# Nearest-neighbour upsampling by two: rows in two blocks of 236 and 276 per partition, ten stores in place of nine, a last load of 9 KB

## The chip, the cores and the metric

The kernel runs on one core of one Trainium2 chip. The metric is device microseconds of that core from launch to end; the profile's span is about 1.4 us shorter (195.8 against 197.17 us before).

## The reference

```python
# x: float32 (16, 64, 64, 64), scale_factor 2; result: (16, 64, 128, 128)
for i in range(new_h):
    for j in range(new_w):
        result[:, :, i, j] = x[:, :, i // scale_factor, j // scale_factor]
```

So 16.78 MB are read and 67.11 MB are written. Each input row of 256 B becomes two equal output rows of 512 B, 1 KiB together.

## The kernel before

All input rows, 65536 of them, are dealt out evenly: partition p owns rows 512p to 512p + 511. One SBUF tile holds the whole input and a window of free space below it. A store's buffer lies either at the start of the tile or just below the input not yet read. VectorE copies 9/16 of a buffer's rows, ACT the rest, and SyncE stores the buffer. All transfers go through one queue.

```python
xp = x.rearrange("b c h w -> (b c h) w").rearrange("(p r) w -> p r w", p=P)
op = out.rearrange("b c (h hd) w -> (b c h) (hd w)", hd=s).rearrange(
    "(p r) w -> p r w", p=P
)
rows = [52, 40, 52, 63, 52, 64, 63, 63, 63]
...
cuts = [0, R // 2, R - 32, R]                       # R = 512
loads = [
    nc.sync.dma_start(out=xt[:, lo:hi], in_=xp[:, lo:hi])
    for lo, hi in zip(cuts, cuts[1:])
]
...
for n, k in enumerate(rows):
    size = k * GROW * W
    at = 0 if n % 2 == 0 else WF + r0 * W - size
    ...
    kv = k * 9 // 16
    nc.vector.tensor_copy(out=u[:, :kv], in_=expanded(r0, r0 + kv))
    nc.scalar.copy(out=u[:, kv:], in_=expanded(r0 + kv, r0 + k))
    store = nc.sync.dma_start(out=op[:, r0 : r0 + k, :], in_=u)
    if n == 0:
        ...   # the first store also waits for the second load: stores begin as the loads end
    r0 += k
```

What the code cuts here leave out: the first load is issued ahead of the opening barrier, and the closing clears of semaphores run beside the last stores. The change doesn't touch them.

Of the kernel before, what the change touches and what calls it, by code (L numbers as in the profile page):

```python
# [153 lines left out]
@with_exitstack  # L154
def kernel(
    ctx: ExitStack,
    tc: tile.TileContext,
    x: bass.AP,
    scale_factor: int,
    out: bass.AP,  # L160
):
    nc = tc.nc
    nc.at_finalize(begin_before_barrier)
    nc.at_finalize(close_early)
    P = nc.NUM_PARTITIONS
    s = int(scale_factor)
    B, C, H, W = x.shape
    R = B * C * H // P
    fdt = x.dtype



    xp = x.rearrange("b c h w -> (b c h) w").rearrange("(p r) w -> p r w", p=P)
    op = out.rearrange("b c (h hd) w -> (b c h) (hd w)", hd=s).rearrange(
        "(p r) w -> p r w", p=P
    )




    rows = [52, 40, 52, 63, 52, 64, 63, 63, 63]
    GROW = s * s
    FREE = 79
    WF = FREE * GROW * W
    assert sum(rows) == R
    mem_pool = ctx.enter_context(tc.tile_pool(name="mem", bufs=1))
    mem = mem_pool.tile([P, WF + R * W], fdt, name="mem")
    xt = mem[:, WF:].rearrange("p (r w) -> p r w", r=R)



    cuts = [0, R // 2, R - 32, R]
    loads = [
        nc.sync.dma_start(out=xt[:, lo:hi], in_=xp[:, lo:hi])
        for lo, hi in zip(cuts, cuts[1:])
    ]

    def expanded(r0, r1):
        return (
            xt[:, r0:r1].unsqueeze(2).unsqueeze(4).to_broadcast([P, r1 - r0, s, W, s])  # L200
        )

    r0 = 0
    before = (0, 0)
# [3 lines that stand above are left out]
        assert at >= before[1] or at + size <= before[0]  # L208
        before = (at, at + size)
        u = mem[:, at : at + size].rearrange(  # L210
            "p (k a w b) -> p k a w b", k=k, a=s, w=W
        )
        kv = k * 9 // 16
        nc.vector.tensor_copy(out=u[:, :kv], in_=expanded(r0, r0 + kv))  # L214
        nc.scalar.copy(out=u[:, kv:], in_=expanded(r0 + kv, r0 + k))  # L215
        store = nc.sync.dma_start(out=op[:, r0 : r0 + k, :], in_=u)  # L216
        if n == 0:
            tc.add_manual_dep(
                store.ins,
                loads[-2].ins.name,  # L220
                mybir.DependencyInfo(
                    mybir.DependencyClass.Sync, mybir.DependencyReason.DATA
                ),
                reason="stores begin as the loads end",
            )
        r0 += k
# [35 lines left out]
```

## Time and profile before

| | before |
|---|---|
| time, median of 3 | 197.17 us (197.1 to 197.4) |
| span | 195.8 us |
| VectorE, ACT busy | 69.6, 51.4 us |
| share of the DMA queue | 99.3% of 16 engines' span |
| moved | 83.89 MB, 428 GB/s over the span |

The prediction below quotes the views.

### The profile page before, as it was taken

How to read it: one execution, taken by the hardware profiler on the slowest of the kernel's cores; microseconds unless marked ns; L12 is line 12 of the kernel's file. 1: busy time of each engine (PE TensorE's matmuls, PEld its weight loads, DVE VectorE, ACT ScalarE, POOL GpSimd, SP SyncE). 2: the span in 40 equal slices, each digit the busy share in tenths (PEclk: the TensorE clock that was granted, in tenths of full speed). 3: DMA queues.
4: the chain of work that ended last, by engine and by line, in shares of the span. 5: the costliest groups of instructions: out<-in, count | busy, mean ns of one | idle time of the engine just before them, and what ended most of it. 6: DMA issues, size and time to landing. Idle time of an engine off the chain costs nothing.

```text
span 195.8 us, 102 instructions
## 1 busy us (share of the span) xinstructions
DVE 69.6 (36%) x9; ACT 51.4 (26%) x10; POOL 0.2 (0%) x4
## 2 busy tenths in 40 slices
DVE  0000596000039289069007205930693079100000
ACT  2000558000036083064920005666000074000000
POOL 0000000000000000000000000000000000000000
DMA  9999889699899999999999899999999999999994
GB/s 428 428 428 428 375 375 562 288 462 522 348 442 410 513 402 468 402 422 422 422 422 522 348 522 428 428 428 428 422 422 422 422 422 435 474 488 488 435 422 211
DMA packets 1728, 83.89 MB, mean 428 GB/s; under 512 B 192, under 2 KB 192, under 8 KB 192
## 3 DMA queue, kind: packets, MB, share of 16 engines
q1 hardware_dynamic: 1728, 83.89, 99.3%
HBM read 16.78 MB, written 67.11 MB: 428 GB/s over the span
## 4 chain that ended last, share of the span: by engine, by line
DMA 67%; DVE 18%; issue 0%; DVEq 0%; SPq 0%
DMA out_dram<-mem 48%; DMA mem<-in_x_dram 19%; DVE mem L214 18%; DVEq L214 0%; SPq L216 0%
## 5 line engine op out<-in xcount | busy, mean ns | idle before, releaser
L214 DVE COPY mem<-mem 128x8960 f32<-128x8960 f32 (+3 forms) x9 | 69.6, 7738 | 97.8 <-DMA out_dram<-mem 75.9
L215 ACT COPY mem<-mem 128x7168 f32<-128x7168 f32 (+2 forms) x9 | 50.1, 5572 | 111.7 <-DMA out_dram<-mem 82.7
L215 ACT ACT_TABLE_LOAD x1 | 1.3, 1283 | 0.8 <-PEq L243 0.8
L243 POOL MEMSET const-bfloat16-1.0<- 128x1 bf16 x1 | 0.1, 101 | 0.0
L243 POOL MEMSET const-uint8-127<- 128x1 uint8 x1 | 0.1, 101 | 0.0
L243 POOL MEMSET const-float32-0.0<- 128x1 f32 x1 | 0.1, 98 | 0.2 <-issue 0.2
L243 POOL MEMSET const-float32-1.0<- 128x1 f32 x1 | 0.1, 98 | 0.0
## 6 DMA issues: line engine op xcount, KB each, us to landing
out_dram<-mem SPq DMA_DIRECT2D x4, 8064.0 KB, 28.4
out_dram<-mem SPq DMA_DIRECT2D x3, 6656.0 KB, 19.7
mem<-in_x_dram SPq DMA_DIRECT2D x1, 7168.0 KB, 38.0
out_dram<-mem SPq DMA_DIRECT2D x1, 5120.0 KB, 29.7
mem<-in_x_dram SPq DMA_DIRECT2D x1, 1024.0 KB, 40.1
mem<-in_x_dram SPq DMA_DIRECT2D x1, 21.8
out_dram<-mem SPq DMA_DIRECT2D x1, 29.9
```

Of the source, the lines that this page charges most:

```text
L214: nc.vector.tensor_copy(out=u[:, :kv], in_=expanded(r0, r0 + kv))
L215: nc.scalar.copy(out=u[:, kv:], in_=expanded(r0 + kv, r0 + k))
L243: nc = _bacc.Bacc("TRN2", target_bir_lowering=False, num_devices=1)
```

## The change

Its intent: with 512 rows per partition, partitions lie 128 KiB apart in the input and 512 KiB in the output, and the 16 DMA engines work at places a power of two apart. If DRAM has trouble with that, two blocks of 236 and 276 rows per partition avoid it. The sizes of stores and loads were fitted to the blocks.

```diff
-    xp = x.rearrange("b c h w -> (b c h) w").rearrange("(p r) w -> p r w", p=P)
-    op = out.rearrange("b c (h hd) w -> (b c h) (hd w)", hd=s).rearrange(
-        "(p r) w -> p r w", p=P
-    )
-    rows = [52, 40, 52, 63, 52, 64, 63, 63, 63]
+    blocks = [236, 276]
+    assert sum(blocks) == R
+    xf = x.rearrange("b c h w -> (b c h) w")
+    of = out.rearrange("b c (h hd) w -> (b c h) (hd w)", hd=s)
+    def block(flat, r0):
+        first = 0 if r0 < blocks[0] else blocks[0]
+        m = blocks[0] if r0 < blocks[0] else blocks[1]
+        rows = flat[first * P : (first + m) * P, :]
+        return rows.rearrange("(p r) w -> p r w", p=P), first
+    rows = [40, 44, 44, 54, 54, 56, 56, 56, 56, 52]
 ...
-    cuts = [0, R // 2, R - 32, R]
-    loads = [ ... in_=xp[:, lo:hi] ... ]
+    cuts = [0, blocks[0], R - 36, R]
+    loads = []
+    for lo, hi in zip(cuts, cuts[1:]):
+        src, first = block(xf, lo)
+        loads.append(
+            nc.sync.dma_start(out=xt[:, lo:hi], in_=src[:, lo - first : hi - first])
+        )
 ...
-        store = nc.sync.dma_start(out=op[:, r0 : r0 + k, :], in_=u)
+        dst, first = block(of, r0)
+        store = nc.sync.dma_start(out=dst[:, r0 - first : r0 - first + k, :], in_=u)
```

More of the change, by code (lines that the diff above doesn't have):

```diff
@@ L188 @@
     xt = mem[:, WF:].rearrange("p (r w) -> p r w", r=R)
-    cuts = [0, R // 2, R - 32, R]
-    loads = [
-        nc.sync.dma_start(out=xt[:, lo:hi], in_=xp[:, lo:hi])
-        for lo, hi in zip(cuts, cuts[1:])
-    ]
+    cuts = [0, blocks[0], R - 36, R]
[5 more added lines that the diff above has]
+        )
     def expanded(r0, r1):
```

## The prediction

> **What bounds the kernel now.** I read the page first (busy shares, the DMA row, the queue), then the order of time, then stretches of it, then the waits of the DMA queue. From the page:
>
> ```profile
> span 195.8 us, 102 instructions
> DVE 69.6 (36%) x9; ACT 51.4 (26%) x10; POOL 0.2 (0%) x4
> ...
> DMA  9999889699899999999999899999999999999994
> ...
> q1 hardware_dynamic: 1728, 83.89, 99.3%
> HBM read 16.78 MB, written 67.11 MB: 428 GB/s over the span
> ```
>
> The two computing engines are busy a third of the span or less. The single DMA queue holds work for 99.3% of it, and moves exactly what the task needs: the input once (16.78 MB) and the output once (67.11 MB). Nothing but the rate of these transfers, and the few microseconds at the ends, is left to win. The view in order of time shows when each store comes free for the copy that waits on it:
>
> ```profile
> 0.00 1.60 SPq L194 DMA_DIRECT2D mem<-in_x_dram  x3
> ...
> 21.86 10.89 DVE L214 COPY mem<-mem 128x7424 f32<-128x7424 f32 x2 [21.86 <-DMA mem<-in_x_dram]
> 29.84 4.03 ACT L215 COPY mem<-mem 128x4608 f32<-128x4608 f32 x1 [2.88 <-DVE mem L214]
> 38.86 128.88 SPq L216 DMA_DIRECT2D out_dram<-mem  x9
> 57.00 5.10 ACT L215 COPY mem<-mem 128x5888 f32<-128x5888 f32 x1 [23.12 <-DMA out_dram<-mem]
> 57.07 7.89 DVE L214 COPY mem<-mem 128x7424 f32<-128x7424 f32 x1 [24.33 <-DMA out_dram<-mem]
> 69.14 6.17 ACT L215 COPY mem<-mem 128x7168 f32<-128x7168 f32 x1 [7.04 <-DMA out_dram<-mem]
> ...
> 119.55 9.49 DVE L214 COPY mem<-mem 128x8960 f32<-128x8960 f32 x1 [10.74 <-DMA out_dram<-mem]
> ...
> 138.88 9.49 DVE L214 COPY mem<-mem 128x8960 f32<-128x8960 f32 x1 [9.84 <-DMA out_dram<-mem]
> ```
>
> The columns are start, duration, instruction, and in brackets the idle time before it and what ended it. The start of each copy marks the landing of a store. So the 64-row store, which runs between 119.55 and 138.88, takes 19.33 us: 64 x 1 KiB x 128 partitions = 8.39 MB, 434 GB/s. The 40-row store takes 69.14 - 57.00 = 12.14 us: 5.24 MB, 432 GB/s. The second load (224 rows of 256 B, 7.34 MB) lands 16.9 us after the first (second landing 38.76, from the end of its piece in the chain below; first 21.86): 434 GB/s.
>
> ```profile
> 0.79 37.97 DMA mem<-in_x_dram
> 38.77 0.02 issue
> ```
>
> That is the key reading: a load, whose partitions lie 128 KiB apart in DRAM, and a store, whose partitions lie 512 KiB apart, run at the same rate within 0.2%. A DRAM conflict that depended on the distance would hardly slow both equally, with read and write directions swapped. Long stretches agree (columns: stretch, length, busy time of DVE, ACT, POOL with counts, clock, DMA share, GB/s):
>
> ```profile
> 0.00:1.00 1.00, 0.00 (x0) 0.21 (x1) 0.20 (x4) 1.00 0.00 0
> 60.00:100.00 40.00, 22.33 (x3) 19.52 (x4) 0.00 (x0) 1.00 1.00 433
> 100.00:150.00 50.00, 23.93 (x3) 12.33 (x2) 0.00 (x0) 1.00 1.00 434
> 60.00:190.00 130.00, 55.75 (x7) 38.02 (x7) 0.00 (x0) 1.00 1.00 433
> ```
>
> Nothing moves in the first microsecond; after that the share is 1.00 and the rate is flat. Short slices of the page swing from 288 to 562 GB/s, but they count whole packets of about 64 KB, so I don't read them as rate. Last, the DMA queue's own waits:
>
> ```profile
> SPq L216 <- DVE mem L214: 125.3, 7, 25.3
> SPq L216 <- DMA mem<-in_x_dram: 37.2, 1, 37.2
> ```
>
> The issuing queue waits 125 us for the copies and 37 us for the second load. That looks like starvation and isn't: each store is issued while the previous one still runs.
>
> **What the Trainium skill says.** (1) "DMA: Bandwidth & Descriptors", "Where 436 GB/s comes from": 16 ports x 32 B x 850 MHz = 435.2 GB/s on the SBUF side. The trace agrees: 433 to 434 GB/s sustained, 99.6% of it. (2) Same page, "Latency and other measured facts", the row on HBM row pitch: DRAM-to-DRAM copies at a pitch of 512 KiB got 207 GB/s per direction, at 2 MiB 164, at 4 MiB 103, and 214 when padded. This is the change's reason: here partitions are 512 KiB apart in the output, and if, as the page has it for such a transfer, an engine serves eight partitions, the engines' places may be megabytes apart. The trace of before doesn't show the loss: at 97% of full rate (207/214) the stores would run near 421 GB/s, and they run at 434. (3) "VectorE: DVE Perf Modes", "Mode 2×_2P — use both read ports for one tensor": a copy in SBUF gets two results per cycle if the outermost dimension is even. The trace agrees: VectorE takes kv = 9k/16 rows of a k-row store; kv = 22 (5632 elements) took 3.08 us, kv = 36 (9216) 4.96 us, but kv = 29 (7424) 7.89 us and kv = 35 (8960) 9.49 us.
>
> **The change part by part.**
>
> *Addresses.* Rows lie in two blocks, so a partition's pitch becomes 59 or 69 KiB in the input and 236 or 276 KiB in the output. Bytes and descriptors per partition keep their kind. Sustained rate: from 434 it could rise at most to 435.2, 0.3% of 190 us = 0.6 us; I expect 0, because loads and stores already agree. Startup: the first load lands at 21.86; its 8.39 MB at the rate of the 64-row store need 19.33 us; so 2.53 us go to start, of which 1.0 us shows no data at all and the rest is the first packets' latency, the spread of the engines and the landing. If the first requests of 16 engines collide in DRAM now, part of that is to be had. I put it at 0 to 0.4 us, middle 0.15: a guess bounded by the 1.5 us.
>
> *Ten stores in place of nine.* The rows are the same 512. Per row the 64- and 40-row stores give (19.33 - 12.14)/24 = 0.300 us, so about 0.12 us is left as fixed cost of a store (12.14 - 40 x 0.300). That difference of wake-ups carries errors of some 0.05 us, so one more store costs 0 to 0.15 us; middle 0.05.
>
> *Loads cut at 236, 476 and 512.* The first load is 20 rows shorter: 20 x 32 KiB = 0.655 MB, 1.5 us at 434 GB/s, so its landing moves from 21.86 to about 20.3. Both first copies (after: kv 22 and 24, at most some 9 us for ACT's pair) end near 29, long before the second load's landing, so nothing is gained. The second landing, the release of the stores, moves from 38.76 to about 38.45 (476 rows in place of 480). The last load grows from 8 to 9 KiB per partition, 1.05 MB to 1.18 MB, 2.4 to 2.7 us: the time that covers the issue of the first store. In before it needed to cover about 1 us (the delay from issue to data seen at the start) plus the spread; it did, as the 130 us afterwards and the sum show: 83.89 MB / 434 = 193.3 plus 2.5 of start = 195.8, the whole span. There is no hole to close: 0.
>
> *Copies.* Fitting the fast pair of VectorE: (4.96 - 3.08)/3584 = 0.524 ns an element plus 0.13 us; the slow pair: (9.49 - 7.89)/1536 = 1.042 ns plus 0.15 us. After: kv = 22, 24, 24, 30, 30, 31 x4, 29, that is 3.08 + 2 x 3.35 + 2 x 4.16 + 4 x 8.42 + 7.89 = 59.7 us in place of 69.6. ACT: 4608 elements 4.03, 7168 6.16, so 0.83 ns an element: 4.03 + 2 x 4.46 + 2 x 5.31 + 4 x 5.49 + 5.10 = 50.6 in place of 50.1. All of it beside transfers: 0 on the path.
>
> Sum: -0.15 (start) + 0.05 (a store more) + 0 + 0 = -0.1 us, so 197.17 becomes about 197.05.
>
> **Rivals.** First: the stores do lose to DRAM conflicts as the skill's row has it, and the change restores 3%: about 154.6 us of stores (67.11 MB at 434) x 0.03 = 4.6 us, about 192.5. Against it: 83.89 MB at the port ceiling of 435.2 is 192.8 us of moving alone; with 2.5 us of start and the 1.4 us between span and measured time (197.17 - 195.8) that makes 196.7. Even with no start at all it would be 194.1, still under 2% (193.2 is the line). So this needs a rate that no stretch shows and the page rules out.
>
> Second: the queue runs dry because stores are smaller. A copy starts when the store two before it lands, and must end while the store just before it runs. Spare time is that store less the copy. Before, tightest at the third store: 12.1 - 7.9 = 4.2 us. After, with 0.3 us per row: third 13.2 - 4.5 = 8.7; fourth 13.2 - 5.3 = 7.9; sixth 16.2 - 8.4 = 7.8; seventh to ninth 16.8 - 8.4 = 8.4; tenth 8.9. All exceed before's 4.2, which sufficed. If it happened anyway, each dry store would cost 1 to 3 us: 198 to 200. The buffers speak neither way: even stores sit at 0, odd ones just below the unread input; ACT's second copy writes over rows that VectorE's first one reads, and that one now takes 3.1 us, less than ACT's first at 4.0, so its wait of 2.88 us goes too.
>
> Third: the new addresses are worse (first rows of neighbouring partitions no longer fall on a regular grid). Every start is still a multiple of 256 B and runs stay 9 to 60 KiB, so at most tenths of a percent: up to 197.6.
>
> Fourth: startup latency was mostly conflicts; then up to 0.7 us goes, 196.5.
>
> **Range and chances.** The middle, rounded down, is 197.0. The repeats of before span 0.3 us, the start term +-0.3, the store term +-0.1; so 196.5 to 197.5 eight times in ten. Faster by 2% means 193.2, below the ceiling's own 194.1: 0.01. Slower by 2% means 201.1, two or more dry stores: 0.01.
>
> **What would show it.** Queue share stays 99% and the flat stretches 433 to 434 GB/s (436 or more: the first rival). First copy near 20.3 us (19.9 or less: a start faster by conflicts removed). Stores released near 38.5; VectorE busy near 59.7 us; copies of 31 rows 8.4 us. Every store issued before the previous one lands; a store whose interval exceeds 0.30 us per row plus 0.15 shows a dry queue. I would be wrong if the rate itself moves.

## The result, and the profile after

| | before | after |
|---|---|---|
| time, median of 6 | 197.14 us (197.1 to 197.4) | 197.3 us (197.22 to 197.42) |
| span of the profiled run | 195.8 us | 195.9 us |
| VectorE, ACT busy | 69.6, 51.4 us | 59.6, 52.1 us |
| first and second load landed | 21.84, 38.76 us | 20.38, 38.52 us |
| all loads landed | 41.23 us | 41.31 us |
| from there to the last store's landing | 154.57 us | 154.56 us |

The ratio of after to before is 1.0006, 95% interval 0.9993 to 1.0018: no difference that these runs resolve. (A ratio is the mean time of one kernel's fast runs over that of the other's fast runs of the same rounds, so not quite the ratio of the medians quoted.) The landings in the table are the last of a transfer's 16 completion records in the trace.

The page of the changed kernel:

```profile
span 195.9 us, 105 instructions
DVE 59.6 (30%) x10; ACT 52.1 (27%) x11; POOL 0.2 (0%) x4
...
DMA  9999999799999999998989989989988988988988
...
q1 hardware_dynamic: 1872, 83.89, 99.3%
HBM read 16.78 MB, written 67.11 MB: 428 GB/s over the span
```

VectorE lost 10 us of work and the last two lines didn't move. The digits of 7 and 8 in the DMA row are no holes: packets of some 57 KB are counted whole in a slice, and the queue's share over the span is the same 99.3%. In order of time (start, duration, instruction, idle time before it and its end):

```profile
0.00 1.60 SPq L204 DMA_DIRECT2D mem<-in_x_dram  x3
...
20.40 6.36 DVE L223 COPY mem<-mem 128x5632 f32<-128x5632 f32 x2 [20.40 <-DMA mem<-in_x_dram]
20.40 8.53 ACT L224 COPY mem<-mem 128x4608 f32<-128x4608 f32 x2 [18.34 <-DMA mem<-in_x_dram]
38.61 133.06 SPq L226 DMA_DIRECT2D out_dram<-mem  x10
53.43 4.46 ACT L224 COPY mem<-mem 128x5120 f32<-128x5120 f32 x1 [24.50 <-DMA out_dram<-mem]
...
129.57 8.42 DVE L223 COPY mem<-mem 128x7936 f32<-128x7936 f32 x1 [8.49 <-DMA out_dram<-mem]
...
146.46 8.42 DVE L223 COPY mem<-mem 128x7936 f32<-128x7936 f32 x1 [8.47 <-DMA out_dram<-mem]
```

The first landing is at 20.4 because the first load is 20 rows shorter. Both first copies of each engine end by 29, and then wait: the stores are released at 38.61, against 38.86 before. The 56-row store between 129.57 and 146.46 takes 16.89 us for 7.34 MB, 434.6 GB/s, where the 64-row store of before had 434. Stretches of the changed kernel:

```profile
0.00:1.00 1.00, 0.00 (x0) 0.21 (x1) 0.20 (x4) 1.00 0.00 0
60.00:190.00 130.00, 49.89 (x7) 37.82 (x7) 0.00 (x0) 1.00 1.00 435
```

The second line is 435 against 433. I put that down to the counting of whole packets at the two edges: the store phase as a whole has the same length to 0.01 us, and run 2, at the old places, shows 435 in the same stretch. And the queue's own waits:

```profile
SPq L226 <- DVE mem L223: 126.1, 8, 19.1
SPq L226 <- DMA mem<-in_x_dram: 36.9, 1, 36.9
SPq L226 <- ACT mem L224: 3.1, 3, 1.1
```

Even row counts make VectorE so fast in the first five stores (3.36 us for 24 rows, 4.16 for 30) that ACT ends last there. The first two are ready long before the loads end; for the other three the queue now waits for ACT. Hence the third line, which is new and costs nothing, since the store before is still under way.

### The profile page after: what moved, and what is told of

Same layout as the page of the kernel before. It is cut to its first block, busy times and chain, and to the rows that moved or that the text cites. A ratio compares the mean times of both kernels' runs of the same rounds, so it can differ in the third digit from the quotient of the medians.

```text
span 195.9 us, 105 instructions
## 1 busy us (share of the span) xinstructions
DVE 59.6 (30%) x10; ACT 52.1 (27%) x11; POOL 0.2 (0%) x4
## 3 DMA queue, kind: packets, MB, share of 16 engines
q1 hardware_dynamic: 1872, 83.89, 99.3%
HBM read 16.78 MB, written 67.11 MB: 428 GB/s over the span
## 4 chain that ended last, share of the span: by engine, by line
DMA 71%; DVE 13%; ACT 3%; issue 0%; SPq 0%; DVEq 0%; ACTq 0%
DMA out_dram<-mem 52%; DMA mem<-in_x_dram 19%; DVE mem L223 13%; ACT mem L224 3%; SPq L226 0%; DVEq L223 0%; ACTq L224 0%
## 5 line engine op out<-in xcount | busy, mean ns | idle before, releaser
L223 DVE COPY mem<-mem 128x7936 f32<-128x7936 f32 (+4 forms) x10 | 59.6, 5970 | 111.7 <-DMA out_dram<-mem 91.3
L224 ACT COPY mem<-mem 128x6400 f32<-128x6400 f32 (+4 forms) x10 | 50.8, 5078 | 107.2 <-DMA out_dram<-mem 82.7
## 6 DMA issues: line engine op xcount, KB each, us to landing
mem<-in_x_dram SPq DMA_DIRECT2D x1, 7552.0 KB, 20.4
```

## The experiments

Theory 1: 434 GB/s is the ceiling of the path between the DMA engines and SBUF; the kernel sits on it from first packet to last, so places in DRAM cannot matter. Theory 2: places did cost something, and the tenth store or the new load sizes gave the gain back. In the runs below the time of before was measured on the same chip in the same rounds: 197.32 us with runs 1 to 4, 197.17 with 5 to 8, 197.21 with 9 and 10, 197.17 with 11 and 12.

### 1 and 2: the changed kernel again, and with the address part alone undone

> The changed kernel once more, so that the other runs of this set have it on the same chip. Theory 1 (the rate of the 16 DMA engines bounds the kernel, and places in DRAM don't matter): 197.2 to 197.4 us, ratio to the kernel before 1.000 to 1.001, sustained rate 433 to 434 GB/s. Theory 2 (the new places do help, and the tenth store or the longer last load gives it back): the same time here; it is told apart by the next run.

> The changed kernel with the address part alone undone: one block of 512 rows per partition, ten stores and the 9 KB last load kept. Theory 1: within 0.2 us of the changed kernel (197.1 to 197.5), store intervals alike to 0.05 us. Theory 2: slower than the changed kernel by what the places bring, 0.3 us or more (197.6 and up), with packets of more than 2.12 us for 56 rows, or a later first landing than 20.4 us.

```diff
-    blocks = [236, 276]
+    blocks = [512]
 ...
-        first = 0 if r0 < blocks[0] else blocks[0]
-        m = blocks[0] if r0 < blocks[0] else blocks[1]
+        first, m = 0, blocks[0]
 ...
-    cuts = [0, blocks[0], R - 36, R]
+    cuts = [0, 236, R - 36, R]
```

The changed kernel: 197.28 us, ratio to before 0.9998 (0.9984 to 1.0011). With the old places: 197.23 us, ratio 0.9997 (0.9985 to 1.001). With the old places, in order of time:

```profile
20.35 6.36 DVE L222 COPY mem<-mem 128x5632 f32<-128x5632 f32 x2 [20.35 <-DMA mem<-in_x_dram]
...
129.53 8.42 DVE L222 COPY mem<-mem 128x7936 f32<-128x7936 f32 x1 [8.49 <-DMA out_dram<-mem]
...
146.41 8.42 DVE L222 COPY mem<-mem 128x7936 f32<-128x7936 f32 x1 [8.46 <-DMA out_dram<-mem]
```

The first landing is no later (20.35 against 20.40), and the 56-row store takes 16.88 against 16.89 us. A packet in these traces is the piece of one partition, moved by one of the 16 engines; in both traces one of 56 KiB takes 2.116 us in the median. The address part is worth nothing that these runs resolve, and theory 2 falls for this kernel.

### 3 and 4: forty short stores, in two blocks and at the old places

> The changed kernel with each store cut into four by rows: 40 stores of 10 to 14 KiB per partition instead of ten, copies untouched. It measures what one more store costs, which the prediction put at 0 to 0.15 us, middle 0.05. From the traces, a packet takes 37.7 ns per KiB plus some 7.5 ns and each engine handles 8 packets per store, so 30 more stores should cost 30 x (0.03 to 0.07) = 0.9 to 2.1 us: 198.2 to 199.4 us. Under 197.6: a store is free. Over 200: a store costs more than the prediction allowed, and the tenth store alone could have hidden a gain of 0.1 us.

> The same 40 short stores, but at the places of the kernel before (one block of 512 rows, 512 KiB from partition to partition). With runs of 10 to 14 KiB the engines change places four times as often, near the 16 KiB runs of the row on pitch in the Trainium skill. Theory 1: as the run with 40 stores in two blocks, within 0.3 us. Theory 2, in the form that a conflict shows only with short runs: slower than that run by 1 us or more (3% of the stores would be 4.6 us).

```diff
-        store = nc.sync.dma_start(out=dst[:, r0 - first : r0 - first + k, :], in_=u)
+        q = [k * j // 4 for j in range(5)]
+        for j in range(4):
+            at0 = r0 - first
+            store = nc.sync.dma_start(
+                out=dst[:, at0 + q[j] : at0 + q[j + 1], :], in_=u[:, q[j] : q[j + 1]]
+            )
 ...
```

In two blocks: 199.61 us, ratio 1.0117 (1.0103 to 1.013). At the old places: 199.57 us, ratio 1.0114 (1.01 to 1.0128). Places don't matter with runs of 10 to 14 KiB either. Thirty more stores cost 199.61 - 197.28 = 2.33 us, 0.078 us each, a little over the 0.9 to 2.1 us that I expected. So the tenth store of the change costs about 0.08 us by this measure, half of the difference between the medians of the result (0.16 us) and below what any of these comparisons resolves. The packet records say much the same: an engine's store packets add up to 154.81 us before and 154.86 us after, 0.05 us more.

### 5: all partitions load the same rows (wrong result)

> Wrong result on purpose: in the changed kernel, all 128 partitions load the same rows, so that all 16 engines read one and the same stretch of DRAM at once[...]. Theory 1 (engines or ports bound, not DRAM): first landing at 20.3 to 20.6 us, second at 38.4 to 38.8, 197.1 to 197.5 us. Theory 2 (the places matter): the loads change by more than 0.5 us, in either direction; if they ran at half rate, the second landing would be near 75 us and the time near 235 us.

```diff
-            nc.sync.dma_start(out=xt[:, lo:hi], in_=src[:, lo - first : hi - first])
+            nc.sync.dma_start(
+                out=xt[:, lo:hi],
+                in_=xf[lo:hi, :].unsqueeze(0).to_broadcast([P, hi - lo, W]),
+            )
```

197.73 us, ratio 1.0027 (1.001 to 1.0043), 0.2 us above the upper end of what theory 1 expected. The landings are at 20.88 and 39.00 us, both 0.2 to 0.3 us above what it expected. The second load took 18.12 us, as in the changed kernel (18.14), and packets of 60 KiB take 2.267 us in the median in both: there the shared rows leave the rate alone. Only the first load moved, and landed 0.5 us later. The first packets of the 16 engines begin at 1.43 us in the mean instead of 1.16, and between 2 and 19 us the engines stand still for 0.57 us in the mean, which they don't in the changed kernel. An engine's first packet is faster (2.32 us in the mean instead of 2.94), most of its later ones slower (2.26 to 2.30 us in rounds 2 to 7 instead of 2.23 to 2.24). Why the first load differs and the second doesn't is not shown.

### 6: each store one unbroken stretch of DRAM (wrong order on purpose)

> Wrong order of the output on purpose: each of the ten stores of the changed kernel writes one unbroken stretch of DRAM, partition after partition (40 to 56 KiB apart)[...]. Theory 1: 197.1 to 197.5 us, store intervals as in the changed kernel (16.90 us for 56 rows). Theory 2 (both the kernel before and the changed one still lose something in DRAM): faster by 0.5 us or more, intervals of 56 rows under 16.85 us.

```diff
-        dst, first = block(of, r0)
-        store = nc.sync.dma_start(out=dst[:, r0 - first : r0 - first + k, :], in_=u)
+        dst = of[r0 * P : (r0 + k) * P, :].rearrange("(p r) w -> p r w", p=P)
+        store = nc.sync.dma_start(out=dst, in_=u)
```

197.46 us, ratio 1.0014 (0.9999 to 1.0029): the same. The stores land 16.90 to 16.92 us apart for 56 rows. So neither kernel has a DRAM loss that these runs resolve.

### 7 and 11: all copies on ACT, and all on VectorE

> ACT does all copies, VectorE none. ACT takes 0.83 ns an element, so a copy of 56 rows takes 12.1 us instead of 8.4, and ACT is busy near 110 us. Theory 1: a copy has the length of the store before it, 13.3 to 16.9 us, and 12.1 fits, with 1.5 us or more to spare at the fourth store (11.7 in 13.3); time 197.1 to 197.5 us. Rival (what counts is the copies' speed, and a queue that just doesn't run dry): 1 us or more slower, with gaps in the DMA share after the fourth store.

```diff
-        nc.vector.tensor_copy(out=u[:, :kv], in_=expanded(r0, r0 + kv))
-        nc.scalar.copy(out=u[:, kv:], in_=expanded(r0 + kv, r0 + k))
+        nc.scalar.copy(out=u, in_=expanded(r0, r0 + k))
```

197.78 us, ratio 1.003 (1.0015 to 1.0045). This was a miss: I expected 197.1 to 197.5. The copies had the expected length (12.14 us for 56 rows, ACT busy 112.4 us with its table load), and the tightest place was where I had put it:

```profile
67.02 11.71 ACT L222 COPY mem<-mem 128x13824 f32<-128x13824 f32 x1 [3.75 <-DMA out_dram<-mem]
80.24 11.71 ACT L222 COPY mem<-mem 128x13824 f32<-128x13824 f32 x1 [1.51 <-DMA out_dram<-mem]
```

```profile
78.00:81.00 3.00, 1.49 (x2) 0.00 (x0) 1.00 0.73 310
```

The first fence is the order of time, the second a stretch of it. The fourth store's copy ends at 78.73, 1.5 us before the third store lands, and that is not enough. From the issue (78.76) to the first data pass 0.84 us (in the records of the transfers the first packets of this store begin at 79.60), while the engines end the third store's data 0.4 to 1.1 us before its landing is seen. By the transfer records the 16 engines stand still for 0.27 us in the mean at 79 us. A second thing follows. Before that moment the engines start a round of packets 0.71 us apart, from first to last; afterwards 0.15 to 0.24 us apart, and from then on a packet of 56 KiB takes 2.123 us in the mean instead of 2.116. The store phase is 0.33 us longer in all (154.94 against 154.61 us in run 1). The rest of the 0.6 us is within the spread of the runs.

When I wrote the next expectation I had not yet seen the hole:

> The changed kernel with all copies on VectorE, none on ACT. The run with ACT alone was 0.6 us slower although no store waited for a copy: its packets took 2.123 us instead of 2.116 for 56 KiB, for a reason that is open. All ten stores have an even number of rows, so VectorE's fast form holds: 14336 elements in 7.6 us, 10 copies busy near 70 us. Theory 1: 197.1 to 197.5 us, packets of 2.116 us. If any kernel with one engine copying disturbs the packets: 2.12 us and more, 197.7 us and up.

```diff
-        nc.vector.tensor_copy(out=u[:, :kv], in_=expanded(r0, r0 + kv))
-        nc.scalar.copy(out=u[:, kv:], in_=expanded(r0 + kv, r0 + k))
+        nc.vector.tensor_copy(out=u, in_=expanded(r0, r0 + k))
```

197.41 us, ratio 1.0015 (1.0002 to 1.0029), within 2% of before and in the expected range; packets of 2.116 us, engines 0.47 us apart to the end, VectorE busy 69.9 us. So it is not one engine copying alone that disturbs the packets. VectorE's copies, 7.6 us for 56 rows, leave no hole. Both engines' speeds are off the path as long as the queue isn't starved, ACT being the first to starve it.

### 8: stores that read half of the partitions (wrong result)

> Wrong result on purpose: each store is two transfers of 64 partitions, and both read partitions 0 to 63, so that all 16 engines work but read from half of the SBUF's partitions. It asks which of the two, the 16 engines or the 16 ports of the SBUF, sets 434 GB/s. If the ports: the stores take twice 154.6 us, the time is near 352 us. If each engine's own rate: ten more stores at 0.08 us (from the run with 40 stores), 198.0 to 198.3 us.

```diff
-        store = nc.sync.dma_start(out=dst[:, r0 - first : r0 - first + k, :], in_=u)
+        for half in (0, P // 2):
+            store = nc.sync.dma_start(
+                out=dst[half : half + P // 2, r0 - first : r0 - first + k, :],
+                in_=u[: P // 2],
+            )
 ...
```

368.85 us. The loads, and then the stores, as stretches:

```profile
5.00:35.00 30.00, 6.36 (x2) 8.49 (x2) 0.00 (x0) 1.00 0.98 423
60.00:340.00 280.00, 53.25 (x8) 42.28 (x8) 0.00 (x0) 1.00 1.00 206
```

In the second line the DMA share is still 1.00 and the rate is 206 GB/s: all 16 engines have a packet in hand, and each takes twice as long (4.457 us in the mean for 56 KiB instead of 2.116). It is a little worse than half, hence 369 and not 352. The bytes and places in DRAM are the same, though written in another order, so the SBUF partitions that a store reads from set the rate here.

One rival has no run of its own: transfers of 64 partitions might be slow by themselves, whichever partitions they read (two that read 0 to 63 and 64 to 127 were not tried). The packet records speak against it. Two of the first 16 packets of these stores, begun at 40.49 and 40.60 us when other engines still ended the loads, took 1.514 us for 40 KiB, exactly as in the changed kernel. Once all 16 engines read the same 64 partitions, nearly all took some 3.19 us. So a packet of such a transfer can run at full rate, and what slows the rest is, by this reading, the sharing and not the form of the transfer. This fits the Trainium skill's section "Where 436 GB/s comes from" ("DMA: Bandwidth & Descriptors"), which calls the 16 SBUF ports the bottleneck, if half of the partitions have half of the ports. And it tells why the change had nothing to win: the bottleneck is on the other side of the transfer.

### 9 and 10: DRAM to DRAM, at the old places and in two blocks (wrong result)

> Wrong result on purpose: no SBUF at all. 32 transfers copy the input four times from DRAM to DRAM, 128 rows of 16 KiB each, at the places of the kernel before (128 KiB apart in the input, 512 KiB apart in the output). This is the case of the Trainium skill's row on pitch: 207 GB/s there, so 67.1 MB in 324 us; about 327 us with start and end. Its twin in two blocks tells whether the places matter on this chip at all.

> Wrong result on purpose: the same 32 DRAM to DRAM transfers at the places of the changed kernel (two blocks of 236 and 276 rows, tiles of 14.75 and 17.25 KiB). If the row of the skill holds here, 214 GB/s instead of 207: about 3% faster than its twin, near 317 us. If the places don't matter even here: within 1% of its twin.

The loads, copies and stores are replaced by 32 transfers that copy the input four times into the output:

```python
for j in range(s * s):
    for t in range(tiles):                       # 8 tiles of one block, 4 of each of two
        lo, hi = m * t // tiles, m * (t + 1) // tiles
        nc.sync.dma_start(
            out=oq[:, j * m + lo : j * m + hi, :], in_=xq[:, lo:hi, :]
        )
```

Old places 206.58 us, two blocks 207.9 us. The page's line on DRAM traffic, first at the old places, then in two blocks:

```profile
HBM read 67.11 MB, written 67.11 MB: 652 GB/s over the span
```

```profile
HBM read 67.11 MB, written 67.11 MB: 649 GB/s over the span
```

The 327 us expected at the old places missed, and so did the 3% gain in two blocks; the other branch, two blocks within 1% of their twin, came true. In the long stretch from 10 to 190 us the two move the same, counted in one direction, first at the old places:

```profile
10.00:190.00 180.00, 0.00 (x0) 1.00 1.00 329
```

```profile
10.00:190.00 180.00, 0.00 (x0) 1.00 1.00 330
```

DRAM serves some 326 GB/s in each direction over the span, 652 together, and the powers of two are not slower: the two blocks take 0.6% longer in all, with tiles of two sizes. The sum is no ceiling for the kernel, which asks 434 GB/s in one direction at a time. Each packet here varies (a 16 KiB packet took 0.61 to 1.60 us), so in these two runs something on the DRAM side probably binds; a 56 KiB store packet of the kernel, always 2.116 us, shows none of that. The runs read the same 16.78 MB four times, and their input lies 128 KiB apart; the skill's row on pitch may differ in both.

### 12: a last load of 2 KB

> The kernel with ten stores at the places of before, and a last load of 2 KB per partition instead of 9 (cuts at 256, 504 and 512). It asks what the cover of the last load is worth, which the prediction put at 0 between 8 and 9 KB. The first store is issued as the second load lands; before, its first data came about 1.4 us later at most, and 1.0 us after issue at the very start. A 2 KB load covers 0.7 us. So a hole of 0.8 to 1.2 us and 198.0 to 198.5 us, if cover is what a last load is for; 197.1 to 197.5 us if it covers nothing.

```diff
-    cuts = [0, 236, R - 36, R]
+    cuts = [0, 256, R - 8, R]
```

204.84 us, ratio 1.0391 (1.0377 to 1.0405), many times what I expected; but it doesn't answer its question. With these cuts the scheduler put the second store ahead of the first, the only one that waits for the loads. In order of time, and in stretches:

```profile
30.37 148.84 SPq L225 DMA_DIRECT2D out_dram<-mem  x10
...
67.97 9.81 ACT L223 COPY mem<-mem 128x5120 f32<-128x5120 f32 x2 [37.63 <-DMA out_dram<-mem]
```

```profile
68.00:73.00 5.00, 3.33 (x1) 4.97 (x2) 0.00 (x0) 1.00 0.00 0
```

The first store, now in second place, lands at 67.94; only then may the third store's copy begin in its buffer (4.47 us on ACT), and no other store is queued. Five microseconds move nothing at all; by the transfer records the engines stand still for 6.0 us in the mean. Another 1.3 us is lost at the end of the loads (last landing 42.51 instead of 41.24), where the last 16 packets of the second load took 2.72 to 3.91 us instead of 2.34, for a reason that is open, and packets of 56 KiB take 2.1225 us after the hole, as in run 7. So this is what a dry queue looks like and costs: the copy, 0.83 us from issue (72.46) to first data (73.29), and the time by which the engines ended their data before the landing. What a last load of 2 KB costs with the stores in order stays open, and so does what 9 KB bring over 8, beyond the nothing that the result shows.

## Why the prediction was right

- **The bound.** "Nothing but the rate of these transfers" held: 99.3% of the span before and after, and a store phase of 154.57 and 154.56 us. The reading that carried it, loads and stores at one rate in spite of different pitches, was confirmed by runs 2, 4, 5 (its second load) and 6, and run 8 points to its cause, the SBUF side of the transfer.
- **Addresses, rate.** Predicted 0, measured 0 (run 2 against run 1).
- **Addresses, start.** Predicted -0.15 us. This step failed. The first landing is at 20.38 and 20.58 us in two traces of the changed kernel and at 20.32 with the old places; there is no gain, and two traces of the same kernel differ by more than the gain that was forecast. The 2.53 us that the prediction gave to the start can be split by the packet records of before: 1.14 us until the engines' first packets begin in the mean, 0.78 us by which these first packets take longer than the later ones (3.20 instead of 2.42 us for 64 KiB), and 0.59 us from the engines' last data in the mean to the landing. In the changed kernel the parts are 1.16, 0.72 and 0.68 us, and with ten stores at the old places 1.12, 0.76 and 0.63. What makes the first packets slow is open; the change of places doesn't remove it. So the fourth rival, a start made of conflicts that the change would remove (196.5 us), falls too.
- **A store more.** Predicted 0.05, measured 0.078 us by run 3 and 0.05 by the packet records. With 0 for the start, the sum is +0.05 to +0.08 us and not -0.1; the result was +0.06% in ratio, some 0.1 us, which agrees but is not resolved from zero. So nothing bears out the forecast gain of 0.1 us, and with a range of 1 us the total hardly tests it; that the total came so near speaks for the bound, not for this sum. A slip on the way: 12.14 - 40 x 0.300 is 0.14 us and not 0.12, and as the difference of two wake-ups it was too coarse to tell either from 0.05.
- **Loads.** First landing about 20.3, measured 20.38; release of the stores near 38.45, measured 38.52 for the landing; no hole at either last load.
- **Copies.** VectorE 59.7 us predicted, 59.6 measured; ACT 50.6, measured 50.8 (without the table load; the prediction's 5.49 us for 25 rows should be 5.52 by its own rate, and the trace has 5.53); 31 rows 8.42, measured 8.42. The rule of the even outermost dimension that the prediction cites foretold which copies would be fast.
- **Rivals.** Conflicts worth 3% are refuted by runs 2 and 6. New places that are worse don't show either (runs 1 and 2). Dry stores don't occur in the change; runs 7 and 12 show that they are real elsewhere, and that the spare time counted there was too generous by about 1.5 us, since it leaves out the time from issue to data and the lead of the data's end over the landing. With 7.8 us to spare it made no difference.

## What to carry to other kernels

Before treating a transfer for its places in DRAM, compare the rate of loads and stores of different pitch in the trace you have. Here they agreed to a fraction of a per cent and the packets of one size nearly all took the same time, and no change of the stores' places moved them. Then the full queue was left alone by the rest: 10 us less VectorE work and other store sizes changed nothing. What lost time was more transfers (0.08 us each), a queue that runs dry, a source that repeats (0.5 us in the first load) and, by far the most, stores that read half of the partitions. Count the spare time of a store to the end of the previous one's data, with about 0.84 us for its own issue, not to the landing.

## What the Trainium skill lacked or had wrong

- "DMA: Bandwidth & Descriptors", "Latency and other measured facts", the row on HBM row pitch: 207 GB/s per direction at 512 KiB, and 214 at 4 MiB padded by 4 KiB. Here DRAM to DRAM copies in runs of 16 KiB, 512 KiB apart in the output and 128 KiB in the input, moved 326 GB/s per direction, and 325 in two blocks off the powers of two. It is not a repeat of the row's test, as far as the row tells its test: the input is read four times, and not at the output's pitch. For stores from SBUF at a 512 KiB pitch no loss shows at all (434 GB/s).
- Same page, "Where 436 GB/s comes from": its note says that for HBM to SBUF transfers the HBM side, about 358 GB/s, binds. As a rule for every case that is too low: with one core at work both loads and stores held 434 GB/s here, and halving the SBUF partitions read brought the stores to 206. The note itself mentions a measured 425 GB/s; it doesn't say beside its rule that one core alone goes past it.
- No page that I read gives the cost of one more store to a queue that is already full: 0.078 us (30 stores more, 2.33 us).
- None tells that after the queue has run dry once, the engines go on in closer step (0.14 to 0.24 us between first and last instead of 0.71 in run 7 and 0.83 in run 12) and packets of 56 KiB take 2.123 us instead of 2.116; cause open.
